# Normalised rows scaled on ScalarE and transposed, instead of multiplied by a diagonal

## The chip, the cores and the metric

One core of one Trainium2 chip runs the whole program in one launch. The metric is device time in microseconds (us), the median of several runs. The core has five engines with a queue of instructions each: TensorE (PE in the rows; PEld is its weight load, which runs beside the products), VectorE (DVE), ScalarE (ACT), GpSimd (POOL) and SyncE (SP, which issues transfers).

## The reference

Two layers of a trunk run over 384 tokens of width 1024: 128 context tokens and 256 latent ones, which have modulations of their own. Cut to what matters here, a layer is:

```python
h   = rmsnorm(x, norm_mix_pre) * (1.0 + sc1) + sh1
mix = mixer(h)                        # w_in, three groups of heads, w_out
x1  = x + g1 * rmsnorm(mix, norm_mix_post)
h   = rmsnorm(x1, norm_ffn_pre) * (1.0 + sc2) + sh2
out = x1 + g2 * rmsnorm(conv_ffn(h), norm_ffn_post)   # w_up, conv, gelu * b, w_down

def rmsnorm(x, g):
    return x * rsqrt(mean(x * x, -1) + EPS) * g
```

The outputs are both token streams and the final states of the mixer. All is in 32-bit floats.

## The kernel before

The tokens lie in three blocks of 128 rows, `x[0]` (context), `x[1]` and `x[2]` (latent), each 128 x 1024 with tokens on the partitions. The projections want the normalised tokens the other way round, with the width on the partitions, and split into a high part that TensorE takes as it is (`hh`) and the rest (`hl`). Weights come from memory, are split likewise (`copy` on ScalarE gives `hi`, a subtraction on VectorE `lo`), and each product of the mathematics is three on TensorE: high by high, high by low, low by high.

The way of one block from one projection to the next is this. The closing products of the block (`w_out_part`, or `down`) fill two banks of PSUM, the second half of the columns last. `residual` squares each bank on ScalarE with a running sum, multiplies by the gate on VectorE, gets the reciprocal root on GpSimd (`rms`) and adds the result to `x[t]` on VectorE. `norm_pre` squares the two halves of the new `x[t]` on ScalarE, takes the root again, and makes a 128 x 128 diagonal of it on VectorE. `norm_P` multiplies `x[t]` by the diagonal, eight products of 128 columns, which scales and transposes in one. `norm_M` evacuates with the scale and shift of the modulation (the first half of the width on ScalarE, the second on VectorE; for block 1 ahead of the second mixer both on ScalarE), and `norm_S` makes `hh` on ScalarE and `hl` on VectorE.

There are three such turns of blocks after the start of the program: from the output projection to the FFN in each of the two layers, and from the first FFN to the second mixer. In a turn the blocks follow each other. Block t's closing products are 24 of 512 columns. `norm_T_after` pins a block's turning behind the product traced just before it on TensorE. In the kernel before, block 0's stands ahead of block 2's 24 closing products and block 1's behind them; block 2's comes later, amid the first products of the next projection (`first_up` in the FFN, `group` in the mixer). In `first_up` the first up-projection `a` is done for block 0 alone (48 products of 128 columns), then block 2 is turned, then part of the second up-projection `b` is done for block 0, then `a` for blocks 1 and 2 (48 products of 256 columns), and then the rest of `b`.

The order of instructions on an engine is fixed when the program is built. A planner takes, at each point of a planned time, the instruction of the lowest priority number whose inputs it holds to be ready. The number is the place in the program text, and what stands under `high_priority(offset=300)`, as `residual`, `norm_pre` and the turning do, counts as 300 places earlier. On the chip each engine then runs its queue in that order and waits where an input is late. The splitting of the next weights carries no such offset.

Of the kernel before, what the change touches and what calls it, by code (L numbers as in the profile page):

```python
# [10 lines left out]
F32 = mybir.dt.float32  # L11
F32R = mybir.dt.float32r
BF16 = mybir.dt.bfloat16
AF = mybir.ActivationFunctionType
# [5 lines left out]
KD = D // 128  # L20
DEPTH = 2
T = 384
# [167 lines left out]
class Trunk:  # L190
# [187 lines left out]
    def setup(self):  # L378
        tc, nc, I, ctx = self.tc, self.nc, self.I, self.ctx
        pool = lambda name, bufs, **kw: ctx.enter_context(tc.tile_pool(name=name, bufs=bufs, **kw))  # L380
        self.cst = pool("cst", 1)
        self.wraw = pool("wraw", 4)
        self.wsp = pool("wsp", 4)
        self.tiny = pool("tiny", 2)
        self.act_p = pool("act", 1)
        cst = self.cst

        load = lambda name, shape: self.get(cst, "c_" + name, shape, I["c_" + name])

        cc = self.get(cst, "cc", [128, KD, 2], I["cc"])  # L390
        self.load = load
        dram = pool("dram", 1, space=bass.MemoryType.DRAM)
        self.xd = dram.tile([T, D], F32, name="xd")
        self.specd = dram.tile([128, 3 * 2 * 2 * HYW], F32, name="specd")
        self.gd = [[dram.tile([2, D], F32, name=f"gd{l}{g}") for g in range(2)] for l in range(DEPTH)]
        self.mhalf = cst.tile([128, 16], F32, tag="mhalf", name="mhalf")
        nc.gpsimd.memset(self.mhalf, -0.5)
        self.ones = cst.tile([128, 128], F32, tag="ones", name="ones")
        nc.gpsimd.memset(self.ones, 1.0)

        th = cst.tile([128, KD, 2], F32, tag="cc_t", name="cc_t")
        self.act(th, cc, AF.Tanh, scale=0.5)
        self.ts(th, th, 0.5, ALU.mult, 0.5, ALU.add)
        self.sil = cst.tile([128, KD, 32], F32, tag="sil", name="sil")
        nc.gpsimd.memset(self.sil, 0.0)
        self.tt(self.sil[:, :, 0:2], th, cc, ALU.mult)
        self.onesel = cst.tile([128, 2, 32], F32, tag="onesel", name="onesel")
        nc.gpsimd.memset(self.onesel, 0.0)
        for r in range(2):
            nc.gpsimd.memset(self.onesel[:, r, r:r + 1], 1.0)  # L410
        self.pe_next = False
        self.modT = [[None] * 3 for _ in range(DEPTH)]
        self.queue = []
        self.xn = {}

    def start(self, fp):

# [324 lines left out]
        t = lambda n: pool.tile([128, KD, T], F32R, tag=n, name=self.nm(n))  # L742
        return t("hh"), t("hl")

    def norm_pre(self, t):

        s2 = self.tiny.tile([128, 2], F32, tag="s2", name=self.nm("s2"), bufs=6)
        for c in range(2):
            jk = self.tmp.tile([128, 512], BF16, tag="junkn", name=self.nm("junk"), bufs=1)
            self.act(jk, self.x[t][:, 512 * c:512 * c + 512], AF.Square, scale=D ** -0.5, accum_out=s2[:, c:c + 1])  # L750
        r = self.rms(s2)
        d = self.tmp.tile([128, 128], F32, tag="diag", name=self.nm("diag"), bufs=3)
        self.ts(d, self.ident, r, ALU.mult)
        self.xn[t] = d
# [5 lines left out]

    def norm_P(self, t, c, ps):
        for k in range(4):
            self.mm(ps[:, 128 * k:128 * k + 128], self.x[t][:, 512 * c + 128 * k:512 * c + 128 * k + 128], self.xn[t])
        return ps

    def norm_E(self, t, c, where, h, ps):
# [601 lines left out]
    def w_out(self, l):  # L1368
        self.h2 = self.split_tile(self.tmp)
        self.wo[3] = self.weights("o", l, 3)  # L1370
        self.load_x(l)
        g = self.gate_rows(l, 0)
        for t in range(NT):
            self.w_out_part(l, t, 3)
        for ch in (0, 1):
            self.wo[ch] = self.weights("o", l, ch)
        for t in range(NT):
            if t == 2:
                self.norm_ffn(l, 0)
            self.w_out_part(l, t, 0)  # L1380
            self.w_out_part(l, t, 1, last=True)
            with self.tc.high_priority(offset=300):
                self.residual(t, self.accs[t], g)
                self.norm_pre(t)

    def norm_ffn(self, l, t):
        self.norm_T_after(t, (l, 2, 0, 1, 1), self.h2, lambda c: self.bank(self.WO[t][c]))
# [2 lines left out]
    def ffn(self, l, g):  # L1390
        nc = self.nc
        with self.tc.tile_pool(name=f"ffn{l}", bufs=2, reuse_waits="tile") as fp:
            hh, hl = self.blocks(self.h2)
# [5 lines left out]
            def up_part(ab, w, tok, order, steps, start=True):  # L1399
                a, b = tok  # L1400
                for n, c, k in steps:
                    x, i = order[n]
                    m = w[k // 4][i].rearrange("p (k n) -> p k n", k=4)[:, k % 4, 128 * c:128 * c + 128]
                    self.mm(ab[c][:, a:b], m, x[k][:, a:b], start and n == 0 and k == 0, n == 2 and k == KD - 1)

            def first_up():

                w = self.weights("u", l, 0, ahead=0)
                a, b = ([self.bank(i)[:, :T] for i in pair] for pair in ((6, 7), (3, 4)))
                steps = self.splits(*self.load_weights())  # L1410
                self.norm_ffn(l, 1)

                up_part(a, w, (0, 128), ((hh, 0), (hl, 0), (hh, 1)), product(range(3), range(2), range(KD)))
                for high, _ in steps:
                    high()
                self.norm_ffn(l, 2)
                with self.after(self.dve, self.scalar):
                    for _, low in steps:
                        low()
                w1 = self.prepped[("u", l, 1)]  # L1420
                up_part(b, w1, (0, 128), ((hh, 0), (hl, 0), (hh, 1)), product((0,), range(2), range(KD)))
                late = [(0, c, k) for ks in (range(4), range(4, KD)) for c in range(2) for k in ks]
                late += product((1, 2), (0,), range(KD))
                late += product((1, 2), (1,), range(KD))
                up_part(a, w, (128, T), ((hh, 0), (hh, 1), (hl, 0)), late)
                gated(0, a)
                with self.after(*self.turned):
                    self.weights("u", l, 1)

                up_part(b, w1, (128, T), ((hh, 0),), product((0,), range(2), range(KD)), start=False)  # L1430
                up_part(b, w1, (0, T), (None, (hh, 1), (hl, 0)), product((1, 2), range(2), range(KD)))
                gated(1, b)
                accs.extend([self.bank(2 * t + c) for c in range(2)] for t in range(NT))

# [5 lines left out]
            def gated(p, ab):  # L1440
                cv = fp.tile([128, T], F32, tag="cv", name=self.nm("cv"))
                self.conv3(cv, ab[0], lambda j: self.pc(l, "fc", 4 * p + j))
                self.turned = self.dve, self.scalar
                ge = fp.tile([128, T], F32, tag="ge", name=self.nm("ge"))
                self.act(ge, cv, AF.Gelu_apprx_tanh)
                self.tt(ge, ge, ab[1], ALU.mult)
                hi = fp.tile([128, T], F32R, tag="gh", name=self.nm("gh"), bufs=5)
                lo = fp.tile([128, T], F32R, tag="gl", name=self.nm("gl"), bufs=5)
                nc.scalar.copy(hi, ge)
                self.tt(lo, ge, hi.bitcast(F32), ALU.subtract)  # L1450
                gs[p] = (hi, lo)
# [3 lines left out]
            def down(c, ts=range(NT)):  # L1455
                if c not in ws:
                    ws[c] = self.weights("d", l, c)
                for t in ts:
                    tok = slice(128 * t, 128 * t + 128)
                    blocks = [(gs[p][0][:, tok], gs[p][1][:, tok], w) for p, w in zip((2 * c, 2 * c + 1), ws[c])]  # L1460
                    self.token_major(accs[t], blocks, c == 0, c == 15)

            first_up()
            for c in range(14):
                up(2 * c + 2)
# [11 lines left out]
            if l + 1 < DEPTH:  # L1477
                self.h1 = self.split_tile(self.act_p)
                self.hh, self.hl = self.blocks(self.h1)
            for t in range(NT):  # L1480
                if t == 2 and l + 1 < DEPTH:
                    self.norm_T_after(0, (l + 1, 0, 1, 0, 0), self.h1, lambda c: self.bank(6 + c))
                down(14, [t])
                down(15, [t])
                with self.tc.high_priority(offset=300):
                    self.residual(t, accs[t], g)
                    for c in range(2):
                        self.store_x(l, t, slice(512 * c, 512 * c + 512))
                    if l + 1 < DEPTH:
                        self.norm_pre(t)  # L1490

    def store_x(self, l, t, cols):
        if l + 1 < DEPTH:
# [83 lines left out]
```

## Time and profile before

| what | value |
|---|---|
| median of 3 runs | 1344.52 us (1343.57 to 1345.69) |
| profiled execution | 1343.04 us, its span 1341.3 us |
| PE busy | 1326.4 us, 99% |
| DVE busy | 890.5 us, 66% |
| ACT busy | 569.1 us, 42% |
| granted TensorE clock, mean | 0.999 of full speed |
| read from memory | 210.06 MB, 161 GB/s over the span |

The span is the time from the first instruction to the last of the profiled execution. Times in rows are us from its start. An engine's busy time counts stretches in which at least one of its instructions runs, and products overlap their neighbours: a product's own duration is longer than the step from one to the next, so the cost of a product is read from the difference of two starts.

### The profile page before, as it was taken

The numbers are of one execution on the slowest core, as the hardware profiler recorded it, in microseconds if no ns is written. First come the engines' busy times: TensorE is split into PE (matmuls) and PEld (weight loads), VectorE is DVE, ScalarE is ACT, GpSimd is POOL, SyncE is SP. The second block draws the span as 40 slices with busy tenths as digits, with TensorE's granted clock in tenths as the row PEclk, the third lists the DMA queues.
The fourth block names the chain that finished last, engine by engine and source line by source line (L and its number), as shares of the span: only waits on it lengthen the run. The fifth ranks groups of instructions, "written<-read, shape, count | busy, mean of one in ns | idle before, by whom it ended". The sixth has DMA issues, their size and how long they took to land.

```text
span 1341.3 us, 19422 instructions
## 1 busy us (share of the span) xinstructions
PE 1326.4 (99%) x7527; PEld 1205.8 (90%) x7527; DVE 890.5 (66%) x1594; ACT 569.1 (42%) x944; POOL 35.2 (3%) x64
## 2 busy tenths in 40 slices
PE   8999999999999999999999999999999999999998
PEld 2788899889998998999889999988999999999997
DVE  5647677577897898889466678656545445445445
ACT  3653344564333333333357544446433333333333
POOL 1100000000000000000000000000000000000000
PEclk9999999999999999999999999999999999999999
DMA  9786624434655665665235332433433333333331
GB/s 353 284 324 244 224 87 131 153 132 167 213 200 177 215 221 177 223 240 174 98 124 178 95 96 87 131 128 143 153 126 126 126 125 126 126 125 127 126 123 50
DMA packets 59101, 217.27 MB, mean 162 GB/s; under 512 B 7214, under 2 KB 9456, under 8 KB 53632
## 3 DMA queue, kind: packets, MB, share of 16 engines
q1 hardware_dynamic: 59008, 216.02, 47.1%
q8 instruction: 59, 0.97, 0.3%
q14 instruction: 34, 0.28, 0.1%
HBM read 210.06 MB, written 5.94 MB: 161 GB/s over the span
## 4 chain that ended last, share of the span: by engine, by line
PE 90%; DMA 5%; DVE 2%; ACT 2%; issue 1%; POOL 0%; SPq 0%; DVEq 0%; POOLq 0%; ACTq 0%
PE b L208 89%; DMA mraw<-in_w_mod 1%; PE b L212 1%; DMA raw<-in_w_up 1%; DMA hi<-in_w_mod 1%; DMA lo<-in_w_mod 1%; DMA raw<-in_w_in_m 1%; ACT hi L278 1%; DVE lo L255 1%; ACT junk L274 0%; DMA c_tri<-in_c_tri 0%; DVE mr L921 0%; DMA w<-in_f_w 0%; POOL rr L291 0%; DVE x L266 0%
## 5 line engine op out<-in xcount | busy, mean ns | idle before, releaser
L255 DVE TENSOR_TENSOR lo<-raw,hi 128x1024 fp32r<-128x1024 f32 (+3 forms) x288 | 320.8, 1128 | 205.9 <-ACT hi L278 202.4
L278 ACT CAST hi<-raw 128x1024 fp32r<-128x1024 f32 (+3 forms) x288 | 275.3, 973 | 402.1 <-PE b L208 369.9
L208 PE MATMUL b<-hh,lo 128*128 128x384 f32 (+1 forms) x1120 | 368.1, 336 | 0.0
L208 PE MATMUL b<-hh,hi 128*128 128x384 f32 (+2 forms) x1120 | 365.2, 335 | 0.0
L208 PE MATMUL b<-hl,hi 128*128 128x384 f32 x1088 | 362.7, 338 | 0.0
L208 PEld LDWEIGHTS b<-hh,lo 128*128 128x128 f32 x1120 | 208.1, 188 | 0.9 <-issue 0.8
L208 PEld LDWEIGHTS b<-hh,hi 128*128 128x128 f32 x1120 | 205.7, 188 | 1.6 <-issue 0.3
L208 PEld LDWEIGHTS b<-hl,hi 128*128 128x128 f32 x1088 | 203.7, 188 | 1.2
L208 PE MATMUL b<-lo,hh 128*128 128x384 f32 (+2 forms) x474 | 164.7, 352 | 1.1 <-DVE lo L255 1.1
L208 PE MATMUL b<-hi,hh 128*128 128x384 f32 (+2 forms) x468 | 164.5, 355 | 0.8 <-ACT hh L1360 0.8
L208 PE MATMUL b<-hi,hl 128*128 128x384 f32 (+2 forms) x468 | 163.1, 352 | 0.0
L266 DVE SCALAR_TENSOR_TENSOR cv<-b,pcol,cv 128x127 f32<-128x127 f32 (+1 forms) x256 | 100.6, 414 | 93.7 <-ACT cv L274 89.2
L208 PE MATMUL b<-lo,gh 128*128 128x512 f32 x384 | 151.4, 394 | 0.0
L208 PE MATMUL b<-hi,gh 128*128 128x512 f32 x384 | 150.8, 393 | 0.0
L208 PE MATMUL b<-hi,gl 128*128 128x512 f32 x384 | 149.8, 390 | 0.0
L274 ACT ACTIVATE cv<-b,pcol 128x384 f32<-128x384 f32 x64 | 43.0, 672 | 178.2 <-PE b L208 178.0
L266 DVE SCALAR_TENSOR_TENSOR macc<-mraw,sil,macc 128x512 f32<-128x512 f32 x168 | 113.2, 745 | 0.0
L208 PEld LDWEIGHTS b<-lo,hh 128*128 128x128 f32 x474 | 89.1, 188 | 6.9 <-DVE lo L255 3.0
L208 PEld LDWEIGHTS b<-hi,hh 128*128 128x128 f32 x468 | 87.9, 188 | 7.9 <-ACT hh L1360 1.5
L208 PEld LDWEIGHTS b<-hi,hl 128*128 128x128 f32 x468 | 88.0, 188 | 6.2 <-issue 2.4
L208 PEld LDWEIGHTS b<-hi,gh 128*128 128x128 f32 x384 | 72.1, 188 | 17.7 <-issue 2.5
L208 PEld LDWEIGHTS b<-hi,gl 128*128 128x128 f32 x384 | 72.1, 188 | 15.6
(242 smaller groups left out, 1208.7 us busy)
## 6 DMA issues: line engine op xcount, KB each, us to landing
raw<-in_w_up SPq DMA_DIRECT2D x128, 512.0 KB, 4.8
mraw<-in_w_mod SPq DMA_DIRECT2D x40, 1024.0 KB, 6.9
raw<-in_w_down SPq DMA_DIRECT2D x64, 512.0 KB, 3.7
raw<-in_w_in_r SPq DMA_DIRECT2D x32, 384.0 KB, 3.7
raw<-in_w_in_m SPq DMA_DIRECT2D x24, 384.0 KB, 4.0
raw<-in_w_out SPq DMA_DIRECT2D x16, 512.0 KB, 4.0
raw<-in_w_in_h SPq DMA_DIRECT2D x12, 512.0 KB, 4.7
mraw<-in_w_mod SPq DMA_DIRECT2D x8, 512.0 KB, 9.0
```

The source lines that it names most:

```text
L208: self.pe = self.nc.tensor.matmul(out, lhsT=lhsT, rhs=rhs, start=start, stop=stop, **kw)
L212: self.pe = self.nc.tensor.transpose(out, in_, self.ident[:n, :n])
L255: self.dve = self.nc.vector.tensor_tensor(o, a, b, op)
L266: self.dve = self.nc.vector.scalar_tensor_tensor(o, a, s, b, op0, op1)
L274: self.scalar = self.nc.scalar.activation(o, a, f, **kw)
L278: self.scalar = self.nc.scalar.copy(o, a)
```

## The change

`norm_pre` gets a switch. With `rows=True` it makes no diagonal: ScalarE copies both halves of `x[t]`, scaled by the reciprocal root, into two new tiles `xs`, and `norm_P` transposes these. It is set for blocks 0 and 1 in the turns to the FFN and for all three in the turn to the second mixer; the start of the program and block 2 in the turns to the FFN keep the diagonal. In all three turns the turning of block 0 moves from ahead of block 2's closing products to between their two halves of 12. And in `first_up` the second up-projection `b` does the products of `hl` by column ranges: 128 columns together with block 0's others, 256 together with those of blocks 1 and 2; only those by the low part of the weights stay at 384 columns, and they come last.

```diff
-    def norm_pre(self, t):
+    def norm_pre(self, t, rows=False):
...
         r = self.rms(s2)
+        self.scaled[t] = rows
+        if rows:
+            self.xn[t] = [self.tmp.tile([128, 512], F32, tag="xs", name=self.nm("xs"), bufs=4) for _ in range(2)]
+            for c, o in enumerate(self.xn[t]):
+                self.act(o, self.x[t][:, 512 * c:512 * c + 512], AF.Copy, scale=r)
+            return
         d = self.tmp.tile([128, 128], F32, tag="diag", name=self.nm("diag"), bufs=3)
...
     def norm_P(self, t, c, ps):
         for k in range(4):
-            self.mm(ps[:, 128 * k:128 * k + 128], self.x[t][:, 512 * c + 128 * k:512 * c + 128 * k + 128], self.xn[t])
+            o = ps[:, 128 * k:128 * k + 128]
+            if self.scaled[t]:
+                self.tp(o, self.xn[t][c][:, 128 * k:128 * k + 128])
+            else:
+                self.mm(o, self.x[t][:, 512 * c + 128 * k:512 * c + 128 * k + 128], self.xn[t])
...
         for t in range(NT):
+            self.w_out_part(l, t, 0)
             if t == 2:
                 self.norm_ffn(l, 0)
-            self.w_out_part(l, t, 0)
             self.w_out_part(l, t, 1, last=True)
             with self.tc.high_priority(offset=300):
                 self.residual(t, self.accs[t], g)
-                self.norm_pre(t)
+                self.norm_pre(t, rows=t < 2)
...
-                up_part(b, w1, (0, 128), ((hh, 0), (hl, 0), (hh, 1)), product((0,), range(2), range(KD)))
+                up_part(b, w1, (0, 128), ((hh, 0), (hl, 0), (hh, 1)), product(range(2), range(2), range(KD)))
...
-                up_part(b, w1, (128, T), ((hh, 0),), product((0,), range(2), range(KD)), start=False)
-                up_part(b, w1, (0, T), (None, (hh, 1), (hl, 0)), product((1, 2), range(2), range(KD)))
+                up_part(b, w1, (128, T), ((hh, 0), (hl, 0)), product(range(2), range(2), range(KD)), start=False)
+                up_part(b, w1, (0, T), (None, None, (hh, 1)), product((2,), range(2), range(KD)))
...
             for t in range(NT):
+                down(14, [t])
                 if t == 2 and l + 1 < DEPTH:
                     self.norm_T_after(0, (l + 1, 0, 1, 0, 0), self.h1, lambda c: self.bank(6 + c))
-                down(14, [t])
                 down(15, [t])
...
                     if l + 1 < DEPTH:
-                        self.norm_pre(t)
+                        self.norm_pre(t, rows=True)
```

## Rows read from the trace of the kernel before

**Rows 1.** The page: busy time of TensorE; the chain's shares by engine.
```profile
PE 1326.4 (99%) x7527; PEld 1205.8 (90%) x7527; DVE 890.5 (66%) x1594; ACT 569.1 (42%) x944; POOL 35.2 (3%) x64
PE 90%; DMA 5%; DVE 2%; ACT 2%; issue 1%; POOL 0%; SPq 0%; DVEq 0%; POOLq 0%; ACTq 0%
```
**Rows 2.** Groups by form on PE: line, operation, tiles, shapes, count | busy us, mean ns.
```profile
L208 PE MATMUL b<-diag,x 128*128 128x128 f32 x192 | 23.8, 278 | 1.1 <-DVE diag L260 0.9 <-ACT hf L274 0.2
```
**Rows 3.** Timeline of PE in W of layer 0: start us, us, what, count.
```profile
277.52 0.40 PE L208 MATMUL b<-hi,hl 128*128 128x512 f32 x1
278.08 2.05 PE L208 MATMUL b<-diag,x 128*128 128x128 f32 x16 [0.16 <-DVE diag L260]
279.89 0.48 PE L208 MATMUL b<-hi,hh 128*128 128x512 f32 x1
...
285.48 1.95 PE L208 MATMUL b<-diag,x 128*128 128x128 f32 x16
...
292.57 2.00 PE L208 MATMUL b<-diag,x 128*128 128x128 f32 x16
294.32 1.98 PE L208 MATMUL b<-hh,hi 128*128 128x128 f32 x16
296.14 2.60 PE L208 MATMUL b<-hh,aside 128*128 128x256 f32 x20
...
301.92 2.05 PE L208 MATMUL b<-hh,hi 128*128 128x256 f32 x16
303.80 2.99 PE L208 MATMUL b<-hh,lo 128*128 128x384 f32 x16
```
**Rows 4.** Timeline of PE where transposes of other tiles stand amid products.
```profile
846.29 0.60 PE L212 MATMUL b<-c_ident,q 128*96 128x128 f32 x4
846.64 0.42 PE L208 MATMUL b<-hi,hh 128*128 128x384 f32 x1
```
**Rows 5.** Timeline of ACT in W of layer 0.
```profile
272.46 0.60 ACT L274 ACTIVATE junk<-b 128x512 bf16<-128x512 f32 x1 [0.70 <-PE b L208]
...
277.95 0.60 ACT L274 ACTIVATE junk<-b 128x512 bf16<-128x512 f32 x1 [0.51 <-PE b L208]
...
279.27 1.51 ACT L274 ACTIVATE hf<-b,modT,modT 128x128 f32<-128x128 f32 x4 [0.63 <-PE b L208]
...
281.56 0.60 ACT L278 CAST hh<-hf 128x512 fp32r<-128x512 f32 x1
282.07 0.63 ACT L274 ACTIVATE junk<-x 128x512 bf16<-128x512 f32 x1
...
282.70 1.65 ACT L278 CAST hi<-raw 128x512 fp32r<-128x512 f32 x3
...
285.90 0.60 ACT L274 ACTIVATE junk<-b 128x512 bf16<-128x512 f32 x1
```
**Rows 6.** Timeline of ACT where it scales another tile by a column.
```profile
257.21 1.04 ACT L274 ACTIVATE mix<-b,pcol 128x384 f32<-128x384 f32 x2
```
**Rows 7.** Windows (W, M): us, busy PE, PEld, DVE, ACT, POOL, clock, DMA, GB/s.
```profile
277.75:285.50 7.75, 7.59 (x42) 6.42 (x42) 6.65 (x16) 6.76 (x18) 1.10 (x2) 1.00 0.00 1
285.50:292.60 7.10, 7.10 (x66) 7.10 (x64) 5.96 (x14) 5.29 (x13) 1.10 (x2) 1.00 0.68 211
...
695.80:703.60 7.80, 7.53 (x41) 6.41 (x41) 6.53 (x16) 6.47 (x18) 1.15 (x3) 1.00 0.19 69
703.60:712.90 9.30, 9.30 (x58) 8.99 (x57) 6.57 (x14) 6.43 (x18) 1.35 (x3) 1.00 0.67 211
```
**Rows 8.** Timeline of PE in M.
```profile
695.56 0.39 PE L208 MATMUL b<-hi,gl 128*128 128x512 f32 x1
696.22 2.05 PE L208 MATMUL b<-diag,x 128*128 128x128 f32 x16 [0.28 <-DVE diag L260]
...
712.89 1.95 PE L208 MATMUL b<-diag,x 128*128 128x128 f32 x16
```
**Rows 9.** Timeline of DVE in W of layer 0: the diagonal of block 0.
```profile
277.74 0.29 DVE L260 TENSOR_SCALAR diag<-c_ident,rr 128x128 f32<-128x128 f32 x1 [0.68 <-POOL rr L291]
```

More of the change, by code (lines that the diff above doesn't have):

```diff
@@ L413, in setup @@
         self.queue = []
-        self.xn = {}
+        self.xn, self.scaled = {}, {}
     def start(self, fp):
```

## The prediction

> **What bounds the kernel now.** I read the page's busy times first: TensorE is busy for 1326.4 of 1341.3 us and makes 90% of the chain that ended last [rows 1]. The rest of the page says nothing on the change, since it acts at three short places: the two turns from output projection into FFN (W, one in each layer) and the turn from the first FFN into the second mixer (M). So I read the timeline of W in layer 0, engine by engine, then M, and looked at W in layer 1 for differences. The reader is to see three things. TensorE has one visible gap in W, ahead of the first diagonal products: 278.08 - 277.52 less one product's 0.23 us is 0.33 us [rows 3]; in M it is 0.66 - 0.23 = 0.43 us [rows 8]; the second W repeats the first, and I take 0.33 again. Elsewhere in the turns product follows product, so a removed product is time only if what it was waiting beside is ready earlier too. And ScalarE, at 42% over the span, is nearly full there: busy 12.05 of 14.85 us between the gap and the third block's diagonal products in W, and 12.90 of 17.10 us in M [rows 7].
>
> **The change, part by part.** I write 0, 1, 2 for the three token blocks and P(t), E(t) for a block's turning on TensorE and its evacuation (scale and shift, high part, low part).
>
> *Transposes for diagonal products.* Before, 12 norms of 8 products make 192 records [rows 2]: two for each product. Sixteen take 279.89 - 278.08 = 1.81 us at block 0 and 294.32 - 292.57 = 1.75 at block 2 [rows 3], 0.11 us a record; I take 1.75. A transpose of the same shape is one record, and four of them take 846.64 - 846.29 = 0.35 us [rows 4], up to 0.44 with the slower step behind them. Eight cost 0.7 to 0.9 us; I take 0.85, so 0.9 us go per block. Changed are blocks 0 and 1 in each W and all three in M: 7 x 0.9 = 6.3 us.
>
> *The first block's turn, 12 products later.* In all three turns P(0) leaves the place where it waits for its diagonal. Two passes that start with the diagonal at 277.74 [rows 9] end at 278.9, 1.6 us before P(0) now stands, so the gaps of twice 0.33 and 0.43 us go, 1.1 together. What is late next is P(1): TensorE reaches it sooner by gap and P(0)'s saving, 1.2 us in W.
>
> *Longer second up-projection.* The products with the low part of the tokens are split in two column ranges: 16 of 384 columns go, 16 of 128 and 16 of 256 come. By their pitch: 1.82/16 = 0.114 us for 128 (294.32 to 296.14), 1.88/16 = 0.118 for 256 (301.92 to 303.80), (2.99 - 0.34)/15 = 0.177 for 384 [rows 3]. So 16 x (0.114 + 0.118 - 0.177) = +0.88 us, twice: +1.75. In exchange there are 32 instead of 16 products that need only block 0 and can stand around P(2).
>
> TensorE alone: -6.3 - 1.1 + 1.75 = -5.65 us. That is W: -1.8 - 0.33 + 0.88 = -1.25 each, and M: -2.7 - 0.43 = -3.1.
>
> *Scaling on ScalarE.* Each changed block gets two passes over 128x512 from SBUF with a column as scale. No row shows one. Nearest is a scale by a column over 128x384: two in 1.04 us [rows 6], so with one's 0.58 us a pitch of some 0.47; in proportion to columns 0.62 at most, and the pitch of the 384 at least. I take 0.57, so 1.15 us a block (bounds 0.94 to 1.24). VectorE loses the diagonal of 0.29 us [rows 9]. Added to ScalarE: 2.3 us in each W, 3.45 in M.
>
> The Trainium skill ("ScalarE: Activation LUTs", Rules for kernel authors) says that a multiplication belongs on VectorE, not ScalarE, and prices the pass (What ACT_TABLE_LOAD costs) at 186 + 93 + 0.833 x 512 ns, less 93 of overlap: an estimate of 0.61 us, which would make the sum below up to 0.6 us dearer over 7 blocks. The two records of rows 6 lie within 0.05 us of its formula, so the trace agrees as far as it shows.
>
> Who waits behind these passes? In W, block 0's scale factor is there at 277.74, where the diagonal starts [rows 9], and block 1's last square is due at 277.95 [rows 5]. Two passes ahead of it push it to 278.9, 0.95 us late; one ahead, 0.4; none, 0. Block 1's statistics and so P(1) shift by that. Next, P(0) ends its first half at 277.75 + 12 x 0.23 + 0.43 = 280.95 (24 products take 5.59 us between 279.89 and 285.48, [rows 3]). From 281.25 on ScalarE has to do block 0's four scale-and-shifts (1.5 us), block 1's two squares of the new rows (282.70 - 282.07 = 0.63 each), block 1's two passes (1.15), block 0's two casts (282.07 - 281.56 = 0.51 each) and block 2's first square (0.6) [rows 5]: 5.55 us, so block 2's last square begins at about 286.8, against 285.90 before, although its products end 1.2 us sooner. From a block's last square to its P the least seen is 272.46 to 278.08 = 5.6 us [rows 3, 5]. So P(2) starts at 292.4, or somewhat later if the order leaves gaps: about where it was (292.57).
>
> The windows say the same: the work of ScalarE up to P(2) becomes 12.05 + 2.3 = 14.35 us of the present 14.85; with 1.5 of its 2.8 us of idle time left over and 0.9 us of the three weight casts at 282.70 [rows 5] put behind P(2), P(2) moves by +0.1. TensorE has 14.85 - 0.33 - 1.8 = 12.7 us to do in that stretch, so it waits for 2.2 us, half ahead of P(1), where nothing is ready, half ahead of P(2), where the 32 products can be drawn in. Then the products of block 0 end at 292.7 + 1.75 + 3.65 - 1.1 = 297.0, +0.85 against 296.14, and what follows them is shorter by 0.95 (16 x 0.177 less 16 x 0.118): W **-0.1 us**. Its bounds: -1.25 if ScalarE delays nothing; +3.2 if the passes add their full 2.3 us to the way to P(2) and the added products fill nothing (2.3 + 0.88). I take -0.1 because the queue's order follows from rows that stand close by.
>
> In M ScalarE's work up to P(2) becomes 12.90 + 3.45 = 16.35 us, TensorE's 17.1 - 0.43 - 1.8 = 14.9. Block 1's evacuation lies wholly on ScalarE there, and the closing weights' casts too. With 1 us idle left of 4.2, P(2) stays within 0.3 us of 712.89; its own 0.9 us are gained, less some 0.35 for E(2), which starts half of P(2) after it and then has fewer products beside it. M **-0.4 us**; bounds -3.1 and +2.5 (all 3.45 on the way, less 0.9).
>
> Sum: 2 x -0.1 - 0.4 = -0.6 us, rounded with the chance that one square gets ahead of the passes (-0.3 in a turn) to **-0.8 us**. The profiled execution took 1343.04 us (span 1341.3 and 1.74 around it); so 1342.2, and as the median of the runs, 1.48 above it, **1343.7 us**. Behind the turns TensorE is the bound, so what is won or lost there stays.
>
> **The rivals.**
> 1. *TensorE's saving stands.* For it: TensorE is 99% busy, and ScalarE still has 2.8 and 4.2 us of idle time in the two windows, more than W's 2.3 and M's 3.45. Against: most of that idle time is waiting inside the chain of squares, which the passes lengthen. If two thirds stand, 1344.5 - 3.8 = 1340.7; all of it, 1338.9.
> 2. *ScalarE's queue becomes the bound, and the time gets longer.* Its place is ScalarE's queue ahead of block 2's squares. The casts of the next weights, behind everything of the norms in order, then also hold up the products of block 0 that should fill the wait. For W: P(2) +0.35 and no filler, +0.35 + 0.95 = +1.3; for M 2.5 us idle left, 16.35 + 2.5 - 17.1 - 0.9 = +0.85. Together +3.4: 1347.9. It decides from where ScalarE keeps over 2 us of idle time in either window. The Trainium skill's rule cited above points this way. Against: the three casts of rows 5 take 1.65 us, and ScalarE has about as much free between block 1's late square, done by 279.5, and 281.25.
> 3. *The change doesn't do what it says:* a transpose of these rows takes as long as the pair. Then +1.75 - 1.1 = +0.65: 1345.2. Rows 4 speak against it, with 128x96 outputs, though, and not 128x128.
>
> **How the numbers follow.** Forecast 0.56, rivals 0.27, 0.11 and 0.06. Under 0.2% (2.7 us) a measurement of this kernel tells no change; forecast and rival 3 lie within it, rival 1 is faster and rival 2 slower: 0.27, 0.62, 0.11. The range 1340.0 to 1347.0 leaves out the better end of rival 1 and most of rival 2, some 0.16; the forecast's own is 1342 to 1345.4.
>
> **What would show it.** Eight records of 0.11 us for P(0) and P(1), 0.9 us less each; P(0) without a gap; two scaling passes of 0.57 us on ScalarE ahead of block 1's second square; a wait of about 1 us ahead of P(1); P(2) within 0.5 us of its old distance from the first close (14.8 us); ScalarE idle for under 2 us between. The prediction is wrong if P(1) starts without a wait or block 2's squares start as soon as its products end (rival 1), or if TensorE waits behind P(1) for a high part or a weight cast (rival 2).

## The result, and the profile after

The change made the kernel slower: 1364.31 us (median of 4 runs, 1362.93 to 1365.23) against 1344.05 us of the kernel before on the same chip (4 runs, 1341.90 to 1345.69), a ratio of 1.0148 with a 95% interval of 1.0133 to 1.0163. The forecast was 1343.7 us with a range up to 1347.0. The profiled execution took 1363.58 us, its span is 1361.8 us: 20.5 us more than before.

The page of the kernel after: busy times, the granted TensorE clock in 40 slices, and the chain's shares, beside [rows 1].
```profile
PE 1331.2 (98%) x7503; PEld 1209.8 (89%) x7503; DVE 888.4 (65%) x1587; ACT 575.7 (42%) x958; POOL 36.5 (3%) x64
PEclk9999999979999999999998999998999999999999
PE 89%; ACT 3%; DVE 3%; DMA 2%; issue 1%; POOL 1%; SPq 0%; DVEq 0%; POOLq 0%; ACTq 0%
```
TensorE runs 24 records fewer and is nevertheless busy 4.8 us longer, and the span grew by 20.5: so TensorE both waits more and takes longer for its work. The clock row has three dips: in slice 9 (272 to 306 us, W of layer 0), slice 22 (715 to 749 us, the end of M) and slice 28 (919 to 953 us, W of layer 1); a slice is 34 us.

The groups by form for the new operations, beside [rows 2]:
```profile
L274 ACT ACTIVATE xs<-x,rr 128x512 f32<-128x512 f32 x14 | 9.3, 714 | 4.3 <-POOL rr L291 4.1 <-POOL mpl L923 0.2
L212 PE MATMUL b<-c_ident,xs 128*128 128x128 f32 x56 | 8.0, 278 | 6.7 <-ACT xs L274 6.7
```
Fourteen passes and 56 transposes, as the change says; and 6.7 us in which TensorE stood still ahead of transposes for `xs`.

TensorE's timeline in W of layer 0, after, beside [rows 3]:
```profile
276.60 0.39 PE L208 MATMUL b<-hi,hl 128*128 128x512 f32 x1
...
279.58 1.03 PE L212 MATMUL b<-c_ident,xs 128*128 128x128 f32 x8
280.37 0.48 PE L208 MATMUL b<-hi,hh 128*128 128x512 f32 x1
...
282.98 0.40 PE L208 MATMUL b<-hi,hl 128*128 128x512 f32 x1
285.63 1.27 PE L212 MATMUL b<-c_ident,xs 128*128 128x128 f32 x8 [2.25 <-ACT xs L274]
287.67 0.77 PE L208 MATMUL b<-hh,aside 128*128 128x128 f32 x5 [0.77 <-ACT hh L278]
288.77 2.61 PE L208 MATMUL b<-hh,aside 128*128 128x128 f32 x11 [0.32 <-ACT hh L278]
291.17 3.62 PE L208 MATMUL b<-hl,aside 128*128 128x128 f32 x16
...
298.00 3.72 PE L208 MATMUL b<-diag,x 128*128 128x128 f32 x16
301.38 2.29 PE L208 MATMUL b<-hh,hi 128*128 128x128 f32 x16
303.50 1.95 PE L208 MATMUL b<-hl,hi 128*128 128x128 f32 x16
```
Three things are to be seen. P(0), at 279.58, has no wait ahead of it and takes 0.79 us to the next product, as forecast. Behind the last closing product TensorE waits: 2.25 us for block 1's scaled rows, then 0.77 and 0.32 us for block 0's high part. And from 288.77 us on products take twice as long: 16 of 128 columns last 3.62 us where they last 1.95 at 303.50, and the diagonal products step from 298.00 to 301.38, 3.38 us, where they took 1.75 [rows 3].

The windows of that stretch, after, beside [rows 7] (columns as there; the last number before DMA share and GB/s is the granted clock):
```profile
284.00:288.00 4.00, 1.60 (x11) 1.17 (x12) 1.37 (x5) 3.50 (x9) 0.55 (x1) 1.00 0.36 131
288.00:292.00 4.00, 3.68 (x19) 3.54 (x19) 3.56 (x8) 3.70 (x11) 0.87 (x1) 0.55 0.42 127
292.00:296.00 4.00, 4.00 (x21) 4.00 (x21) 2.48 (x7) 1.41 (x4) 0.55 (x1) 0.50 0.33 135
...
304.00:308.00 4.00, 4.00 (x36) 4.00 (x36) 2.91 (x5) 0.00 (x0) 0.00 (x0) 1.00 0.29 81
```
TensorE is busy for 1.60 of the 4 us from 284; behind that the granted clock is 0.50, that is 1.2 GHz instead of 2.4. Read in windows of 1 us, it stands there from 288.4 to 302.0, for 13.6 us. In the windows of before it was 1.00 throughout.

ScalarE's timeline, after, beside [rows 5]:
```profile
276.81 1.34 ACT L274 ACTIVATE xs<-x,rr 128x512 f32<-128x512 f32 x2 [0.86 <-POOL rr L291]
278.05 0.58 ACT L274 ACTIVATE junk<-b 128x512 bf16<-128x512 f32 x1
...
278.62 0.58 ACT L274 ACTIVATE junk<-b 128x512 bf16<-128x512 f32 x1
...
284.86 1.33 ACT L274 ACTIVATE xs<-x,rr 128x512 f32<-128x512 f32 x2 [0.49 <-POOL rr L291]
...
287.01 0.61 ACT L278 CAST hh<-hf 128x512 fp32r<-128x512 f32 x1
...
288.10 0.61 ACT L278 CAST hh<-hf 128x512 fp32r<-128x512 f32 x1
```
ScalarE idles 0.86 us for block 0's reciprocal root, makes block 0's two passes, and only then squares block 1's two banks. Block 1's last square begins 278.62 - 276.60 = 2.02 us behind its last product, where before it began 277.95 - 277.52 = 0.43 us behind it [rows 3, 5]: 1.59 us late. Block 0's first cast (287.01) comes behind block 1's passes and block 2's first square, the second (288.10) behind both squares. VectorE's diagonal for P(2), before and after:
```profile
291.88 0.29 DVE L260 TENSOR_SCALAR diag<-c_ident,rr 128x128 f32<-128x128 f32 x1 [0.41 <-POOL rr L291]
```
```profile
293.92 0.29 DVE L260 TENSOR_SCALAR diag<-c_ident,rr 128x128 f32<-128x128 f32 x1 [0.41 <-POOL rr L291]
```
From the start of block 1's last closing product that is 14.36 us before (277.52 to 291.88) and 17.32 after (276.60 to 293.92): 2.96 us later.

M, after: TensorE, beside [rows 8],
```profile
711.92 1.27 PE L212 MATMUL b<-c_ident,xs 128*128 128x128 f32 x8 [2.19 <-ACT xs L274]
713.96 0.99 PE L208 MATMUL b<-aside,hh 128*128 128x400 f32 x4 [0.77 <-ACT hh L278]
...
717.32 0.99 PE L208 MATMUL b<-aside,hh 128*128 128x400 f32 x4 [1.45 <-ACT hh L278]
721.72 1.70 PE L208 MATMUL b<-hi,hh 128*128 128x400 f32 x4 [3.40 <-ACT hh L278]
...
728.71 1.04 PE L212 MATMUL b<-c_ident,xs 128*128 128x128 f32 x8
```
and ScalarE just before the longest of these waits ends:
```profile
719.82 1.33 ACT L274 ACTIVATE xs<-x,rr 128x512 f32<-128x512 f32 x2 [0.23 <-POOL mpl L923]
721.06 0.60 ACT L278 CAST hh<-hf 128x512 fp32r<-128x512 f32 x1
```
The cast for which TensorE waits 3.40 us stands in ScalarE's queue behind block 2's two passes, whose rows are not used before 728.71.

The balance, from the timelines: the length of a turn is from the start of block 1's last closing product to the first product of the projection after the turn (in W the first `hh,hi` of 384 columns of the third pair of up-projections, 309.45 before and 317.60 after; in M the first `hi,hh` of 384 columns).

| us | before | after | difference |
|---|---|---|---|
| W, layer 0 | 31.93 | 41.00 | +9.07 |
| M | 25.12 | 33.06 | +7.94 |
| W, layer 1 | 31.94 | 40.80 | +8.86 |
| rest of the span | | | -5.4 |
| span | 1341.3 | 1361.8 | +20.5 |

Of the rest, the second FFN (from the end of its W to the end of the span) went from 393.1 to 388.6 us: -4.5 us in a place where nothing was changed.

### The profile page after: what moved, and what is told of

Read it like the earlier page. It is cut to its first block, busy times and chain, and to the rows that moved or that the text cites. A ratio compares the mean times of both kernels' runs of the same rounds, so it can differ in the third digit from the quotient of the medians.

```text
span 1361.8 us, 19388 instructions
## 1 busy us (share of the span) xinstructions
PE 1331.2 (98%) x7503; PEld 1209.8 (89%) x7503; DVE 888.4 (65%) x1587; ACT 575.7 (42%) x958; POOL 36.5 (3%) x64
## 4 chain that ended last, share of the span: by engine, by line
PE 89%; ACT 3%; DVE 3%; DMA 2%; issue 1%; POOL 1%; SPq 0%; DVEq 0%; POOLq 0%; ACTq 0%
PE b L208 88%; PE b L212 1%; DMA raw<-in_w_up 1%; ACT junk L274 1%; DVE lo L255 1%; POOL rr L291 1%; DMA raw<-in_w_in_m 1%; ACT xs L274 1%; DVE x L266 1%; ACT hi L278 1%; ACT hf L274 0%; DMA modbm<-in_mod_bm 0%; DMA w<-in_f_w 0%; DVE mr L931 0%; DVE yg L255 0%
## 5 line engine op out<-in xcount | busy, mean ns | idle before, releaser
L208 PE MATMUL b<-hl,hi 128*128 128x384 f32 (+2 forms) x1120 | 363.2, 333 | 0.0
L208 PEld LDWEIGHTS b<-lo,gh 128*128 128x128 f32 x384 | 72.1, 188 | 14.8
```

The source lines that it names most:

```text
L208: self.pe = self.nc.tensor.matmul(out, lhsT=lhsT, rhs=rhs, start=start, stop=stop, **kw)
```

## The experiments

Ten kernels, in the order run. Theory A: ScalarE's passes delay block 1's squares, TensorE runs dry behind the closing products, and its clock falls. Theory B: the later place of block 0's turning is to blame. Theory P: the split of `b` (the second up-projection in the turn) is what makes the products of the FFN behind it step faster. A1 and A2 tell apart, within A, the order of the passes and the amount of work. N and O, last, are about what in the split matters. W0 and W1 are W of layer 0 and of layer 1. Turn lengths in this table are read as above, from the one profiled execution of each kernel; "step" is that of 384-column products in the second FFN.

| kernel | ratio (95%) | W0 | M | W1 | step, ns |
|---|---|---|---|---|---|
| move only | 1.0007 (0.9994 to 1.0020) | 31.77 | 25.40 | 31.76 | 176.7 |
| scaling only | 1.0066 (1.0044 to 1.0088) | 32.95 | 33.04 | 32.95 | 176.7 |
| scaled on VectorE | 0.9986 (0.9969 to 1.0002) | 32.97 | 25.66 | 32.95 | 173.4 |
| kept busy | 1.0065 (1.0043 to 1.0086) | 35.38 | 32.73 | 35.39 | 173.4 |
| split only | 0.9961 (0.9946 to 0.9975) | 32.72 | 25.15 | 32.72 | 173.4 |
| move and split | 0.9957 (0.9945 to 0.9970) | 32.54 | 25.40 | 32.55 | 173.4 |
| passes behind squares | 1.0108 (1.0085 to 1.0131) | 39.39 | 32.89 | 37.92 | 173.4 |
| VectorE, no split | 1.0038 (1.0024 to 1.0051) | 32.17 | 26.95 | 32.17 | 176.7 |
| swap only | 1.0007 (0.9998 to 1.0017) | 31.92 | 25.17 | 32.03 | 176.7 |
| split, old end | 0.9967 (0.9954 to 0.9980) | 32.77 | 25.12 | 32.78 | 173.4 |

**Move only.** The kernel after, without its scaling and its split:
```diff
-                self.norm_pre(t, rows=t < 2)
+                self.norm_pre(t, rows=False)
...
-                        self.norm_pre(t, rows=True)
+                        self.norm_pre(t, rows=False)
...
-                up_part(b, w1, (0, 128), ((hh, 0), (hl, 0), (hh, 1)), product(range(2), range(2), range(KD)))
+                up_part(b, w1, (0, 128), ((hh, 0), (hl, 0), (hh, 1)), product((0,), range(2), range(KD)))
```
(and the second half of `b` likewise).

> Only the move: block 0 turns amid block 2's closing products, every norm keeps its diagonal, the second up-projection is as before. Theory A (ScalarE's two passes delay block 1's squares, TensorE idles, and then runs 12 us at half its clock): no pass, so block 1's diagonal is there in time; the gap of 0.33 us ahead of P(0) goes, no wait over 0.5 us at P(1), granted clock 1.00 behind it: 1342 to 1345 us. Theory B (the later place of block 0 is to blame: its evacuation meets block 1's squares on ScalarE): TensorE waits 2 to 3 us behind P(1) and the clock falls: 1355 to 1364 us.

Measured: 1345.24 us against 1345.01. The two W are 0.16 and 0.18 us shorter, M is 0.28 longer. B falls as a cause by itself.

**Scaling only.** The kernel before with `rows=` as in the change; block 0's turning stays ahead of block 2's closing products, `b` as before.

> Only the scaling on ScalarE and the transposes: block 0 turns at its old place, the second up-projection is as before. Theory A: the two passes now lie on the way to P(0) too, so 1.2 us of wait there (0.33 before) and the rest, 1 to 2 us, at P(1); whether the clock falls with the waiting split in two is open: 1346 us if it holds, 1355 to 1362 if it falls. Theory B: no harm without the move, each transposed block saves 0.9 us: 1339 to 1342 us.

Measured: 1353.67 us, +8.7. M carries nearly all of it (33.04, as after); each W only +1.0. TensorE in its W of layer 0, the two places that wait for the passes:
```profile
279.55 1.27 PE L212 MATMUL b<-c_ident,xs 128*128 128x128 f32 x8 [0.59 <-ACT xs L274]
...
287.81 0.66 PE L212 MATMUL b<-c_ident,xs 128*128 128x128 f32 x4 [1.09 <-ACT xs L274]
```
With P(0) in its old place the waits lie on both sides of the 24 closing products, block 0's high part is made under these, and the clock stays at 1.00 in both W. So scaling alone (+1.0) and move alone (-0.2) don't add up to W's +9.07, nor with the split's 0.79 (below): as the timelines read, the move puts P(0)'s evacuation, P(1)'s wait and the first products in one place. Move and scaling without the split were not run together.

**Scaled on VectorE.** The whole change, with one line of it different:
```diff
-                self.act(o, self.x[t][:, 512 * c:512 * c + 512], AF.Copy, scale=r)
+                self.ts(o, self.x[t][:, 512 * c:512 * c + 512], r, ALU.mult)
```


> The change whole, but VectorE does the scaling of the rows (two multiplications by the column instead of two ScalarE passes). Theory A: ScalarE's queue is that of before, the wait at P(1) shrinks from 2.4 to under 1 us (the scaling itself stays on the way), no fall of the clock: 1343 to 1348 us. Theory B: as the change, 1360 to 1365 us, as the place of block 0 is the same.

Measured: 1342.91 us, the same as before, and 21 us less than the change. Its passes on VectorE, and TensorE's window that answers to 284 to 288 us above:
```profile
283.37 0.88 DVE L260 TENSOR_SCALAR xs<-x,rr 128x512 f32<-128x512 f32 x2 [0.34 <-POOL rr L291]
```
```profile
284.00:288.00 4.00, 3.56 (x30) 3.27 (x30) 3.56 (x9) 4.00 (x12) 0.87 (x1) 1.00 0.31 101
```
Two passes take 0.88 us in place of ScalarE's 1.33, and they are out of ScalarE's queue. The waits in that W shrink to 0.46 us (P(1)), 0.44 (high part) and 0.76 (P(2)), and the clock stays.
```profile
283.91 1.09 PE L212 MATMUL b<-c_ident,xs 128*128 128x128 f32 x8 [0.46 <-DVE xs L260]
```
Same transposes, same places, same split: what costs the 20 us is on which engine the rows are scaled.

**Kept busy.** The change with 14 products of constants in each W, 10 ahead of P(1) and 4 behind it (their results are used nowhere); M as in the change.
```diff
+                self.spin = self.bank(6)
+                self.keep_busy(10)
                 self.norm_ffn(l, 1)
+                self.keep_busy(4)
```


> The change whole, with 14 products of constants added in each of the two turns to the FFN (10 ahead of P(1), 4 behind it) that fill TensorE's waits and give nothing to the result. If the half clock behind those turns follows from the waits: clock 1.00 behind them, 5 to 6 us less for each, 1352 to 1355 us. If the clock has another cause, or costs nothing: 1364 us, or up to 3 us more.

Measured: 1353.60 us. The block 0 products again, and two windows:
```profile
291.07 1.44 PE L208 MATMUL b<-hh,aside 128*128 128x128 f32 x11 [0.29 <-ACT hh L278]
...
300.18 1.95 PE L208 MATMUL b<-hl,hi 128*128 128x128 f32 x16
```
```profile
284.00:288.00 4.00, 3.92 (x19) 2.01 (x18) 2.81 (x8) 3.22 (x9) 0.55 (x1) 1.00 0.31 106
...
292.00:296.00 4.00, 4.00 (x37) 3.94 (x36) 3.37 (x8) 2.95 (x9) 0.78 (x2) 1.00 0.74 262
```
The queues and waits for ScalarE are those of the change, but TensorE isn't idle, and the clock stays at 1.00. From the eleven products by block 0's high part to the low part's products of `b` this kernel takes 300.18 - 291.07 = 9.11 us, the change 303.50 - 288.77 = 14.73: the half clock alone costs 5.6 us in that W, net of a wait of 0.47 us ahead of P(2) that only this kernel has. The other 35.38 - 31.93 = 3.45 us are the waits (which the constant products fill), net of what the transposes save and the split costs.

**Split only.** The kernel before with nothing but the column ranges of `b`:
```diff
-                up_part(b, w1, (0, 128), ((hh, 0), (hl, 0), (hh, 1)), product((0,), range(2), range(KD)))
+                up_part(b, w1, (0, 128), ((hh, 0), (hl, 0), (hh, 1)), product(range(2), range(2), range(KD)))
...
-                up_part(b, w1, (128, T), ((hh, 0),), product((0,), range(2), range(KD)), start=False)
-                up_part(b, w1, (0, T), (None, (hh, 1), (hl, 0)), product((1, 2), range(2), range(KD)))
+                up_part(b, w1, (128, T), ((hh, 0), (hl, 0)), product(range(2), range(2), range(KD)), start=False)
+                up_part(b, w1, (0, T), (None, None, (hh, 1)), product((2,), range(2), range(KD)))
```


> Of the change only the column ranges of the second up-projection's products, in both turns to the FFN. Theory P (in the change, and in the two runs with this part, the up-projections of the last FFN step at 0.173 us a product, in the kernel before and the two runs without it at 0.177; this part puts the products behind it at the faster step): the turns 0.9 us longer each, the FFNs 4 to 6 us shorter together, 1340 to 1342 us. Rival (the step goes with the scaling or the move, or is chance): 1345 to 1347 us.

Measured: 1339.39 us against 1344.28, 0.4% faster and clear of the noise. Each W is 0.79 us longer, close to the forecast's 0.88; but the products of the FFN behind it step faster. The first and the last of the 96 products of one pair of up-projections in the second FFN, before:
```profile
1099.39 0.34 PE L208 MATMUL b<-hh,hi 128*128 128x384 f32 x1
...
1116.18 0.33 PE L208 MATMUL b<-hh,lo 128*128 128x384 f32 x1
```
and after (the kernel with the split alone has the same step):
```profile
1097.61 0.34 PE L208 MATMUL b<-hh,hi 128*128 128x384 f32 x1
...
1114.08 0.34 PE L208 MATMUL b<-hh,lo 128*128 128x384 f32 x1
```
16.79 / 95 = 176.7 ns before and 16.47 / 95 = 173.4 ns after, in each of the 15 pairs behind W of layer 1. Behind W of layer 0 the first five of 15 pairs differ in the same way; from the sixth pair on both steps come in kernels with either `b`, so there it isn't the split that decides. In the profiled executions the split costs 0.79 us in each W and gives back 1.6 us between the first W and M (384.55 for 386.11) and 4.8 us behind the second W (388.3 for 393.1): -4.8 in all, which is the gain measured.

**Move and split.** The kernel after with `rows=False` in both places.

> The change with every norm's diagonal kept: the move and the split second up-projection, no pass on ScalarE and no transposes. Theory A (ScalarE's passes make the loss): no wait over 0.5 us, clock 1.00 in the turns to the FFN; with theory P 1340 to 1342 us, without it 1345 to 1347. If the split or its meeting with the move were part of the loss: over 1350 us.

Measured: 1339.30 us: the two edits that don't touch ScalarE are worth 5 us, nearly all by the split. With the one before it the fastest kernel here.

**Passes behind squares.** The change, with block 0's two passes put behind block 1's squares of sums on ScalarE, out of the planner's hand (`residual` of block 1 calls `scale(0)` behind its two squares):
```diff
+        if t == 1 and self.scaled[0] and type(self.xn[0]) != list:
+            with self.after(self.scalar):
+                self.scale(0)
```


> The change whole, but block 0's two passes are pinned behind block 1's two squares of its sums instead of ahead of them. ScalarE does the same work. Theory A1 (the loss is the order: the passes hold up block 1's chain by 1.6 us): P(1) waits under 1 us instead of 2.4, 1 to 1.5 us of wait is left ahead of block 0's high part, no half clock behind the turns to the FFN: these turns at 32.5 to 34 us (31.9 before, 41.0 in the change), in all 1343 to 1350 us. Rival A2 (the amount of work on ScalarE): waits of 4 us in all and the half clock stay, 1358 to 1364 us.

Measured: 1359.81 us. TensorE in W of layer 0, and the window:
```profile
284.54 1.27 PE L212 MATMUL b<-c_ident,xs 128*128 128x128 f32 x8 [0.23 <-ACT xs L274]
286.92 0.77 PE L208 MATMUL b<-hh,aside 128*128 128x128 f32 x5 [1.11 <-ACT hh L278]
288.02 2.61 PE L208 MATMUL b<-hh,aside 128*128 128x128 f32 x11 [0.32 <-ACT hh L278]
```
```profile
284.00:288.00 4.00, 2.36 (x15) 1.48 (x13) 1.66 (x4) 4.00 (x11) 0.00 (x0) 0.97 0.32 116
288.00:292.00 4.00, 3.98 (x19) 3.98 (x19) 3.56 (x9) 3.69 (x11) 0.87 (x1) 0.50 0.62 208
```
P(1)'s wait is gone (0.23 us in place of 2.25), so the order of the passes did cause that wait; but the wait for block 0's high part grew from 0.77 to 1.11 us, ScalarE is busy for the whole 4.00 us of that window, and the clock falls all the same. A1 holds for one wait, A2 for the turn. In both orders block 0's casts stand behind all four passes; an order with the casts ahead of block 1's passes was not run, so how much is the amount of work and how much the place of the casts is not told apart.

**VectorE, no split.** The change scaled on VectorE, `b` as before.

> The move, and the scaling done by VectorE with transposes; the second up-projection as before. With theory P: the turns to the FFN 0.9 us shorter than with the split (32.1 for 33.0), the FFNs back at the slower step: 1344 to 1347 us. Without it: 1340 to 1342 us.

Measured: 1349.83 us (12 runs, 1346.42 to 1353.69); the step is 176.7 ns again. The split thus gives back 7 us here, more than the 4.9 by itself. By the two profiles, whose spans are 8.3 us apart, the products behind the turns account for 1.6 and 4.8 us less the split's own 1.6; the rest lies in M (26.95 us here, 25.66 with the split) and in the mixer behind it (2.1 us). In M both kernels wait 0.64 us for P(1), and then for a high part; the kernel with the split first, this one behind it, with a window of it:
```profile
705.85 1.00 PE L208 MATMUL b<-hi,hh 128*128 128x400 f32 x4 [2.07 <-ACT hh L278]
```
```profile
706.77 1.00 PE L208 MATMUL b<-hi,hh 128*128 128x400 f32 x4 [2.06 <-ACT hh L278]
```
```profile
709.00:711.00 2.00, 2.00 (x8) 1.98 (x7) 1.56 (x5) 1.97 (x6) 0.80 (x2) 0.50 0.71 209
```
The waits are the same, but here the clock is at 0.50 from 708.2 to 711.6 us, and with the split it stays at 1.00 through M. So the same waits once brought the half clock and once did not; what decides between the two was not found.

**Swap only, and split with the old end.** The kernel before with the last 32 products of `b` in the change's order, unsplit; and the split, with the products by the weights' low part ahead of the last ones of `hl`, as before:
```diff
-                up_part(b, w1, (0, T), (None, (hh, 1), (hl, 0)), product((1, 2), range(2), range(KD)))
+                up_part(b, w1, (0, T), (None, (hl, 0), (hh, 1)), product((1, 2), range(2), range(KD)))
```
```diff
-                up_part(b, w1, (128, T), ((hh, 0), (hl, 0)), product(range(2), range(2), range(KD)), start=False)
-                up_part(b, w1, (0, T), (None, None, (hh, 1)), product((2,), range(2), range(KD)))
+                up_part(b, w1, (128, T), ((hh, 0),), product((0,), range(2), range(KD)), start=False)
+                up_part(b, w1, (0, T), (None, (hh, 1)), product((1,), range(2), range(KD)))
+                up_part(b, w1, (128, T), (None, None, (hl, 0)), product((2,), range(2), range(KD)))
```
(the second diff is against the split of the change.)

> The kernel before with nothing changed but the order in which the second up-projection b of the turn into the FFN does its last 32 products of 384 columns: the 16 by the low part of the tokens (hl, hi) come ahead of the 16 by the low part of the weights (hh, lo), as in the change, but not split by columns, so there is no product more. Theory N (the split itself, that is the 16 added products in b, takes the products that follow from a step of 176.6 to one of 173.4 ns): nothing happens, the step in the second FFN stays at 176.6 ns and the time at 1344.3, within 1 us. Theory O (what decides is the kind of products that b ends with): the step goes to 173.4 ns from the last products of b on, and the second FFN loses 4.5 us; without the split's own cost of 0.8 us in each turn the time is 1338 to 1340.

> The kernel before with b split by columns as in the change, but with the order at its end as before: the products by the low part of the weights (hh, lo, 384 columns) come ahead of those of hl over blocks 1 and 2 (256 columns), so that b ends with hl. Theory N: the step of the second FFN is 173.4 ns and the time that of the split alone, 1339.4, within 1 us. Theory O: the step stays at 176.6 ns, and the split's own cost of 0.8 us in each turn is added to 1344.3: 1346, within 1 us.

Measured: 1345.76 and 1339.57 us against 1344.73. First and last of the same 96 products, swap only:
```profile
1104.52 0.34 PE L208 MATMUL b<-hh,hi 128*128 128x384 f32 x1
...
1121.31 0.33 PE L208 MATMUL b<-hh,lo 128*128 128x384 f32 x1
```
split with the old end:
```profile
1101.49 0.34 PE L208 MATMUL b<-hh,hi 128*128 128x384 f32 x1
...
1117.96 0.34 PE L208 MATMUL b<-hh,lo 128*128 128x384 f32 x1
```
176.7 and 173.4 ns: N holds and O falls, although the swap alone came out 1.0 us above the kernel before, just past N's margin and within the noise (0.9998 to 1.0017). What takes the following products to the faster step is the split itself, in either order. The number of products elsewhere doesn't do it: the step stays with 56 records fewer (scaling only) and with 28 more (kept busy). The number of products in `b` and their columns change together in it; which of the two does it was not tried.

## Why the prediction was wrong

**The step that failed** is the account of waiting, in the part on scaling on ScalarE: "it waits for 2.2 us, half ahead of P(1), where nothing is ready, half ahead of P(2), where the 32 products can be drawn in", from which followed W -0.1 and M -0.4. Two things in it were wrong. The waits themselves are dearer: with the clock held at 1.00 W is 3.45 us longer (kept busy), not 0.1 shorter; how that came is told below. And it held a product's step to be the same behind a wait as without one. The granted clock stood at 1.00 in every window of [rows 7], so nothing in the trace of before priced a wait beyond its own length; the prediction did not ask. In the change some 3.3 us of waits in W (2.25 + 0.77 + 0.32) were followed by 13.6 us at 0.50, and that added 5.6 us more (40.80 - 35.39 = 5.4 in the second W): 11 of the 26 us that the three turns lost.

**Where TensorE waits.** The place was right: ScalarE's queue, P(1) first. The sizes were not. The passes step at 0.62 us (two from 276.81 to 278.05) where 0.57 was taken; two of them were to push block 1's last square by 0.95 us; it came 1.59 late. The forecast put only that square behind the passes; the planner put both there, with 0.86 us of ScalarE idle ahead of them, since in its order the passes came first. Behind that the reciprocal root on GpSimd took 0.93 us in place of 0.55. So P(1) waited 2.25 us, not about 1. P(2), which was to move by +0.1 us, had its diagonal 2.96 us later; TensorE, slowed by the half clock, came to it later still, and with the clock held it is what TensorE waits for there, 0.47 us. The forecast filled 1.3 us of ScalarE's idle time with passes; but ScalarE still idles for 0.86 and 0.49 us ahead of the two pairs of passes, for the reciprocal roots that scale them, so the idle time was not free.

**What fills the wait.** The 32 products of block 0 were to be drawn into a wait ahead of P(2). But block 0's high part itself was late: its casts stand behind block 1's passes and one or both of block 2's squares. The prediction listed these casts among ScalarE's 5.55 us ahead of block 2's last square and followed only P(2) through that list, not the cast that releases the filler. It named this sign itself ("if TensorE waits behind P(1) for a high part"), and that is what came.

**M** was to lose 0.4 us and became 7.9 longer. With all three blocks' passes on ScalarE and block 1's evacuation there too, TensorE waits 2.19 us at P(1) and 0.77, 1.45, 3.40 and 0.35 us for high parts, together 8.2; and the clock is at 0.50 from 718.5 to 725.3 us. The bound of +2.5 counted the passes' own 3.45 us once; here they delay three casts one after the other. The loss in M is there without the move (33.04) and gone with VectorE (25.66), so it is the passes. How it divides between waits and clock was not measured apart; an estimate from the rows is that the clock takes some 1.7 us of it, since the twelve products of 400 columns from 721.72 take 3.90 us to the next at 725.62, and twelve such took 2.20 us before (706.12 to 708.32).

**The rivals.** What happened is the second rival's mechanism, given a chance of 0.11, with a price of +3.4 us. Its waits alone, with the clock held, cost 3.45 us in one W, where it said 1.3. Its condition, ScalarE's "over 2 us of idle time", hangs on where the window is cut: it is busy for 13.26 of 15.40 us from 276.6 to 292, and for 12.92 of 14.85 from 277.75 to 292.6. The first rival (TensorE's saving stands) fails by the same waits; the third by 0.79 us for P(0).

**What was right:** the transposes (0.79 us where 0.85 was taken), the gaps ahead of P(0), the passes' price within 0.05 us, and the split's own cost (0.79 for 0.88 us in each W). **The split's other side was wrong:** the prediction took the products behind the turn as they were ("what is won or lost there stays"). They step 3.3 ns faster: 15 x 96 of them in the second FFN, 4.7 us by that, 4.5 measured, and in the first FFN 5 x 96, 1.6 us by that. With the split the whole is -4.9 us, not +1.75; without the gain in the second FFN the change would have lost some 25 us, by estimate.

The Trainium skill ("TensorE: Matmul & The Clock Gate", HAM oscillation) describes kernels whose waits between products bring the half clock. The trace agrees here, with 1.00 falling to 0.50 behind the waits at 283 to 288 us, the longest of them 2.25 us; the prediction did not weigh that page. The rule that it did weigh, a multiplication on VectorE instead of ScalarE ("ScalarE: Activation LUTs", Rules for kernel authors), is borne out: the same change with the pass on VectorE takes 1342.91 us.

## What to carry to other kernels

Before work is moved to an engine that is half idle over the span, write out its queue through the stretch concerned and follow every result that the busiest engine waits for, the filler's inputs as well as the transposed rows: in a chain of dependent steps the idle time isn't free to use. Price a wait of TensorE amid dense work by more than its length: here 3.3 us of waits cost another 5.6 us of half clock, though waits don't bring it every time. And try the parts of a change apart: of these three edits the split was worth -5 us, the move nothing, and the scaling on ScalarE hid that.

## What the runs showed of the hardware

- Behind the waits of one turn, products took twice their time for 13.6 us, with TensorE busy for 3.68 of the 4 us from 288 and then for 4.00 of 4.00; filling the waits with products of constants kept the granted clock at 1.00. The half level came in all three turns of the change and of the kernel with the passes behind the squares, in M alone of the two kernels with ScalarE's passes whose W wait less or are filled (scaling only, kept busy), for some 3 us in M of one of the two kernels scaled on VectorE, whose waits in M are the same, and in no turn of the kernels that scale by the diagonal.
- The Trainium skill ("TensorE: Matmul & The Clock Gate", Part 4: PE-mode transpose) says that the full clock does not engage for transposes. In the kernel scaled on VectorE the same 16 transposes stand in W and the granted clock is 1.00 in all of 276 to 296 us, so they don't cost it here by themselves.
- Short stretches at 0.50, some 3 us each, also come between 734 and 752 us, in the mixer behind M, in the profiled runs of seven kernels (move only, scaling only, scaled on VectorE, passes behind squares, VectorE without split, swap only, split with the old end), and not in those of before, after, kept busy, split only and move and split. They follow no part of the change; what brings them was not looked into.
- Products of 384 columns step at one of two levels, 173.4 or 176.7 ns. In all twelve kernels profiled, at the first pairs behind W of layer 0 and at all 15 pairs behind W of layer 1, a split `b` goes with the first level and an unsplit one with the second. From the sixth pair behind W of layer 0 on, both levels come with either `b` (before: 173.4 in the sixth to ninth pair, after: 176.7). What in TensorE makes two levels is open.
- GpSimd's reciprocal root over 128x1 took 0.55 to 0.56 us in W of layer 0 before, and 0.93 us at 280.19 and 0.87 at 289.25 after, where VectorE makes a 128x512 subtraction from 280.02 to 280.70 and from 289.02 to 289.71. The Trainium skill ("GPSIMD Engine Reference", Key points) says that the two share their access to SBUF; the trace agrees as far as this goes.
- A scaling pass over 128x512 steps at 0.62 us on ScalarE (two from 276.81 to 278.05; one lasts 0.71) and on VectorE two last 0.88 us from start to end, against 1.34.
